# A hybrid decoder block on one core: 28 gate tiles as fourteen pairs by seven block products, recurrence operands read from DRAM, the inverse of four heads at a time

## The chip, the core and the metric

The kernel runs on one core of one Trainium2 chip. TensorE (PE) multiplies matrices into PSUM; VectorE (DVE), ScalarE (ACT) and GpSimd (POOL) do the elementwise work; SyncE (SP) issues nearly all DMAs. Each engine runs its own instructions in the order in which the program wrote them, and waits for the others by semaphores. The metric is the device time of one execution in microseconds, as a median over runs.

## The reference, cut to what matters

One block works on 1024 tokens of width 1024. All of it is float32.

```python
h = rms_norm(x, norm_w) * (1 + scale) + shift            # scale, shift, gate from c @ ada_w
proj = h @ w_in                                           # one projection, split in columns:
(qa, ka, va, za, beta_in, a_in, qb, kb, vb, zb, ga, gb) = split(proj)
qa, ka, va = split(silu(causal_dwconv(concat(qa, ka, va))))
o_a = gated_delta_rule(l2(qa), l2(ka), va, g, beta)       # 8 heads of 128, a recurrence over chunks
y_a = (rms_norm(o_a) * silu(za)) @ w_proj_a
o_b = dilated_window_attention(qb, kb, vb)                # 12 heads of 64, three groups
y_b = (o_b * softmax_over_groups * silu(zb)) @ w_proj_b
merged = sigmoid(ga) * y_a + sigmoid(gb) * y_b
out = rms_norm(x + gate * (merged @ w_out), final_norm_w)
```

The four quantities `za`, `zb`, `ga` and `gb` are the gates. They need nothing but `h` and their columns of `w_in`, and they are used late.

## The kernel before

**Products.** A float32 product is made of three: each operand is split into a high part `hi`, rounded to the type float32r, and the rest `lo`, and `three` (line 557) sums hi·hi, hi·lo and lo·hi. The activations stand transposed in eight pairs of tiles `hT[kk]` of 128 x 1024 (128 features by all tokens). A projection tile is 128 columns of `w_in`: for each of eight `kk` six matmuls of 512 columns, 48 in all, into one of two PSUM tiles `pj` of two banks. There are 66 such tiles: 8 each of q, k, v and z of mixer A (`qA`, `kA`, `vA`, `zA`), 6 each of `qB`, `kB`, `zB`, and 16 of the gates `gA` and `gB`. The three value tiles `vB` have the tokens in the rows and are made of 192 matmuls of 272 or 256 columns each. Behind the projections, `tail_products` (line 1532) multiplies by P_A (8 tiles of 48), P_B (8 of 36) and W_o.

**Weights.** `w_load` (line 521) brings a tile into one of two buffers `wr`; `w_split` (line 529) makes `hi` on ACT and `lo` on DVE in two of six tiles `wh`; the raw buffer is free again when both are made.

**Order.** The program is written by a planner. Every piece of work is a generator, a stream; `Sched` (line 103) keeps a clock for each engine with estimated durations (`book`, line 120) and lets the ready stream of the lowest number write its next instructions. The stream `projections` (line 724) has the number 99: it fills PE whenever no other stream has something ready. So the order on every engine is fixed before the run. `ORDER` (line 27) gives the projection tiles in four rounds of two heads each, with `g` for a gate tile; then come `qB` and `kB`, the six `zB` and what is left of the gates.

**Space.** 34 `big` tiles of 128 x 1024 hold `hT` (16), the operands of the heads in work, and the rest; six `mid` tiles of 128 x 512 and four one-bank PSUM tiles `sb` serve the smaller streams. `Slots.get` waits for a free tile.

**Mixer A.** For a head: `conv` (k, q, v), `d_stream` (decay), `k_stream` (k by rows, scaled: `KP`), `n_stream` (the 8 triangular matrices of 128 x 128), `inv_stream` (line 949), `merge_stream` (line 977), `q_stream`, and `rec_stream` (line 1107). `inv_stream` inverts the 32 x 32 diagonal blocks of two heads, 64 partitions, by 31 multiplications and 31 subtractions on DVE; `merge_stream` joins them to the inverse `TT`, of which there are two. `rec_stream` goes through eight chunks, each with matmuls that need the result of the one before, and reads k, q, `KP`, v and the matrix `AT` from tiles in SBUF. `turn` (line 1082) moves tokens back to the free axis through DRAM.

**Mixer B.** `attn_group` (line 1271) loads a group's values, waits for the group before, and has two workers go through eight `attn_unit` (line 1191). `combine` (line 1316) takes the softmax over the groups when all three are done and `ev_yas[7]` is set; `apply_gate` multiplies with the gate; `yb_split` makes the parts for P_B.

At the start `FIRST` (line 24) is 2: the tiles k0 and k1 are computed while `h` is being formed, and `ORDER` goes on with q0 and B0.

## Time and profile before

| what | us |
|---|---|
| median of 3 runs (1300.20 to 1302.47) | 1302.35 |
| the profiled execution | 1300.81 |
| its span, first to last instruction | 1299.0 |
| PE busy | 1261.6 |
| DVE, ACT, POOL busy | 690.9, 494.3, 145.4 |
| mean granted TensorE clock | 0.994 of full speed |

A page of the profile gives the busy time of each engine, the span in 40 slices of 32.5 us with the busy share in tenths, the chain of work that ended last, followed back from the last instruction, and groups of instructions with their count, busy time, mean duration and the idle time ahead of them. Every operation is recorded by one helper (line 96), so that groups are told apart by the names of their tiles: `pj<-big,wh` is a projection matmul, `wh<-wr` the splitting of a weight, `sb<-` the small streams. Matmuls overlap in the pipeline: the mean duration of one is longer than the distance between two. Other views are lists of waits by engine, tables of busy time in stretches of the span, and the timeline, in which a row is start, duration, engine and instruction, with a count where several follow each other.

### The profile page before, as it was taken

The page shows a single profiled execution, that of the slowest core. Times are in us where ns is not written, and L with a number is a line of the kernel's source. Part 1 is how long each engine was busy: PE and PEld are TensorE (multiplying, and loading weights), DVE is VectorE, ACT ScalarE, POOL GpSimd, SP SyncE. Part 2 cuts the span into 40 slices and gives each one's busy share as a digit, 9 for nine tenths or more (in the row PEclk, how much of TensorE's full clock was granted, in tenths as well). Part 3 has the DMA queues.
Part 4 walks back from the last instruction along what each step waited for, and adds up shares of the span by engine and source line. Part 5 has one row for each costly group of instructions (what it writes and reads, how often), then busy time and mean ns, then how long its engine had stood idle before and what let it go on. Part 6 is the DMA issues. An engine that isn't in the chain of part 4 may idle for free.

```text
span 1299.0 us, 18858 instructions
## 1 busy us (share of the span) xinstructions
PE 1261.6 (97%) x7386; PEld 1049.0 (81%) x7386; DVE 690.9 (53%) x1437; ACT 494.3 (38%) x1054; POOL 145.4 (11%) x97
## 2 busy tenths in 40 slices
PE   5799899999999999999999999999999999999997
PEld 3698678988888988888888888777777888888886
DVE  6766682377763468843778533232322147645433
ACT  5637312455234362234542242453536342222211
POOL 4601200023000221001310002000000000002400
PEclk9899999999999999999999999999999999999999
DMA  9335532163321433231522226211100257333422
GB/s 362 120 123 179 95 93 58 33 197 94 95 70 40 149 125 93 78 102 33 179 74 73 82 66 194 66 35 65 35 33 33 83 187 208 102 127 117 156 95 89
DMA packets 76138, 137.65 MB, mean 106 GB/s; under 512 B 30193, under 2 KB 43921, under 8 KB 76050
## 3 DMA queue, kind: packets, MB, share of 16 engines
q1 hardware_dynamic: 75906, 136.20, 33.2%
q8 instruction: 58, 0.95, 0.3%
q14 instruction: 30, 0.25, 0.1%
q10 hardware_dynamic: 144, 0.26, 0.1%
HBM read 105.84 MB, written 30.59 MB: 105 GB/s over the span
## 4 chain that ended last, share of the span: by engine, by line
PE 82%; issue 7%; DVE 6%; DMA 3%; POOL 1%; ACT 1%; SPq 0%; POOLq 0%; DVEq 0%; ACTq 0%
PE pj L96 69%; PE sb L96 13%; DVE big L96 4%; DMA big<-in_x_dram 1%; DMA vtd<-big 1%; DVE wh L96 1%; POOL big L96 1%; DVE mod L96 1%; DMA big<-grow 0%; ACT big L96 0%; DVE mid L96 0%; DMA big<-otd 0%; SPq L96 0%; POOL mo L96 0%; DMA otd<-big 0%
## 5 line engine op out<-in xcount | busy, mean ns | idle before, releaser
L96 PE MATMUL pj<-big,wh 128*128 128x512 f32 x3840 | 941.8, 398 | 11.2 <-POOL big L96 6.4
L96 PEld LDWEIGHTS pj<-big,wh 128*128 128x128 f32 x3840 | 706.3, 189 | 157.5 <-POOL big L96 7.8
L96 ACT ACTIVATE wh<-wr 128x1024 fp32r<-128x1024 f32 (+3 forms) x96 | 95.6, 996 | 316.1 <-PE pj L96 292.4
L96 DVE TENSOR_TENSOR wh<-wr,wh 128x1024 fp32r<-128x1024 f32 (+3 forms) x93 | 115.5, 1243 | 148.1 <-ACT wh L96 147.9
L96 ACT ACTIVATE big<-big 128x1024 f32<-128x1024 f32 (+1 forms) x61 | 64.5, 1059 | 147.2 <-DVE big L96 115.7
L96 PE MATMUL pj<-wh,big 128*128 128x256 f32 (+2 forms) x702 | 109.5, 307 | 0.0
L96 PEld LDWEIGHTS pj<-wh,big 128*128 128x128 f32 x702 | 95.9, 189 | 5.2 <-DVE big L96 0.2
L96 DVE SCALAR_TENSOR_TENSOR big<-pj,cw,big 128x1023 f32<-128x1023 f32 (+2 forms) x66 | 84.4, 1279 | 1.8 <-ACT big L96 0.3
L96 PEld LDWEIGHTS sb<-sq,big 128*128 128x128 f32 x464 | 62.6, 191 | 4.4
L96 PE MATMUL sb<-sq,big 128*128 128x128 f32 x464 | 65.5, 274 | 0.0
L96 DVE TENSOR_TENSOR big<-big,big 128x1024 f32<-128x1024 f32 (+3 forms) x40 | 55.2, 1388 | 15.1 <-ACT big L96 13.0
L96 ACT ACTIVATE big<-pj 128x1024 f32<-128x1024 f32 (+1 forms) x56 | 51.7, 923 | 21.3 <-PE pj L96 21.2
L96 ACT ACTIVATE mid<-sb 128x384 f32<-128x384 f32 (+5 forms) x75 | 34.1, 461 | 66.8 <-PE sb L96 66.4
L96 POOL TENSOR_TENSOR wh<-wr,wh 128x1024 fp32r<-128x1024 f32 x3 | 8.4, 2785 | 399.0 <-ACT wh L96 399.0
L96 ACT ACTIVATE mid<-mid,sta 128x128 f32<-128x128 f32 (+1 forms) x96 | 42.2, 441 | 25.5 <-DVE sta L96 25.4
L96 DVE COPY big<-sb 128x256 f32<-128x256 f32 (+1 forms) x32 | 12.4, 389 | 74.0 <-PE sb L96 73.9
L96 DVE SCALAR_TENSOR_TENSOR sq<-sq,gsm,sb 128x128 f32<-128x128 f32 x48 | 16.5, 345 | 63.2 <-PE sb L96 61.8
L96 PE MATMUL pj<-big,big 128*128 128x512 f32 x210 | 49.1, 389 | 0.0
L96 ACT ACT_TABLE_LOAD x29 | 37.2, 1283 | 28.8 <-DVE big L96 23.9
L96 PE MATMUL sb<-big,big 128*128 128x128 f32 (+4 forms) x365 | 45.5, 316 | 2.0 <-DVE big L96 2.0
L96 PEld LDWEIGHTS pj<-big,big 128*128 128x128 f32 x210 | 39.4, 188 | 8.2
L96 DVE TENSOR_TENSOR mid<-big 64x31 f32<-64x31 f32 (+15 forms) x124 | 41.1, 332 | 9.0 <-POOL big L96 5.6
(124 smaller groups left out, 1086.3 us busy)
## 6 DMA issues: line engine op xcount, KB each, us to landing
wr<-in_w_tiles_dram SPq DMA_DIRECT2D x64, 512.0 KB, 3.9
big<-in_ada_w_dram SPq DMA_DIRECT2D x24, 512.0 KB, 9.0
big<-in_x_dram SPq DMA_DIRECT2D x16, 512.0 KB, 5.0
gd<-big SPq DMA_DIRECT2D x16, 512.0 KB, 5.0
big<-gd SPq DMA_DIRECT2D x16, 512.0 KB, 4.7
big<-grow SPq DMA_DIRECT2D x8, 512.0 KB, 5.6
vtd<-big SPq DMA_DIRECT2D x8, 512.0 KB, 3.0
big<-vtd SPq DMA_DIRECT2D x32, 128.0 KB, 3.8
```

The lines of the kernel that those rows point to most:

```text
L96: r = f(*a, **k)
```

## The change

**Pairs.** The gate tiles `zA` (8), `zB` (6) and the first 14 of `gA`, `gB` are made two at a time (`two`), each pair by a form of Strassen's algorithm (`pair`). The weights of two tiles and the activations are cut into 2 x 2 blocks, A and B: halves of the features by tile, and halves of the features by halves of the tokens. Seven products of 128 x 512 x 512 give the four output blocks, where S1 = A21 + A22, S2 = S1 - A11, S3 = A11 - A21, S4 = A12 - S2, T1 = B12 - B11, T2 = B22 - T1, T3 = B22 - B12, T4 = B21 - T2. A product is four steps of three matmuls, 84 for the pair. `w_combine` makes the sums of the weights, `h_blocks` those of the activations once; T1 takes the place of B12 in `hT` and B12 comes back from DRAM after the last pair. `pair_out` adds the products up, and the outputs, through Silu or Tanh, go to DRAM (`z_d`, `gate_d`).

**Order.** The pairs come after 15 entries of `EARLY` (`a` is a `qB` and a `kB` tile) and ahead of `ORDER`, which has the other heads, the other attention tiles and two plain gate tiles; `named` and `ATT` hold attention group 0 until head 3's last chunk is loaded, 1 until k6, 2 until v7. The first tile behind k0 and k1 is B0.

**DRAM.** k, q, `KP` and `AT` are written to `rk_d`, v to `vr_d`, the triangular matrices to `nr_d`; `rec_stream` reads one chunk of 128 x 512 at a time into the two halves of one tile (`chunks`, two ahead). The q and k of mixer B go through `qb_d` and `kb_d`, read half a group at a time (`attn_second`), attention outputs through `og_d`; `yb_split`, two streams, reads them with the gates and takes over `apply_gate`; `combine` no longer waits for `ev_yas[7]`.

**Other.** `inv_stream` takes four heads, 128 partitions, twice instead of four times. The low part of a plain weight tile is made by POOL in place of DVE. The load of the last eight `ada_w` tiles begins when `h` is done. In `Sched.book` the estimates change (for a large matmul `n / 2.4 + 13.4` in place of `max(107, n / 2.4 + 2)`, and larger constants for DVE, ACT, POOL and the DMAs, a smaller one in `chain`).

The core of the diff:

```diff
-ORDER = (
-    "q0 B0 v0 q1 v1 z0 g g z1 g g B1",
-    "k0 k1 q0 v0 z0 g v1 q1 z1 g g B2",
-    "k0 k1 q0 v0 z0 g q1 v1 g g z1 g",
-    "k0 k1 q0 v0 z0 g q1 v1 z1 g g g",
-)
+EARLY = "k0 k1 B0 k2 k3 q0 q1 q2 q3 v0 v1 v2 v3 a0 a1"
+ORDER = "k4 k5 k6 k7 q4 q5 q6 q7 v4 v5 B1 a2 v6 v7 a3 B2 a4 a5 g14 g15"
+HALVES = (slice(0, 512), slice(512, 1024))
+PRODUCTS = (("A11", "B11"), ("S2", "T2"), ("S1", "T1"), ("A12", "B21"), ("S3", "T3"), ("S4", "B22"), ("A22", "T4"))
+BLOCKS = ("B11", "T2", "T1", "B21", "T3", "B22", "T4")
+ATT = ("c3", "k6", "v7")
+BLK = "q1"
+NTWO = 14
...
             yield
-            dve.tensor_tensor(u.lo, u.raw, u.hi.bitcast(F32), op=OP.subtract)
+            pool.tensor_tensor(u.lo, u.raw, u.hi.bitcast(F32), op=OP.subtract)
             wr.put()
             S.set(u.ev)
             yield S.now()
...
+    def w_combine(u):
+
+        half = u.n // 2
+
+        def part(src, names, hi, lo):
+            n = half * len(names)
+            act.activation(hi[:, 0:n], src, AF.Copy)
+            yield
+            dve.tensor_tensor(lo[:, 0:n], src, hi[:, 0:n].bitcast(F32), op=OP.subtract)
+            for q, name in enumerate(names):
+                sl = slice(q * half, q * half + half)
+                u.part[name] = (hi[:, sl], lo[:, sl])
+                S.set(u.ev[name])
+            if names[0] == "S2":
+                big.put()
+                big.debt += 1
+            if names[0][0:2] in ("S3", "S4"):
+                wr.put()
+
+        def begin(src, *names):
+            if len(names) == 2:
+                hi = yield from wh.get(F32R, shape=[P, u.n])
+                lo = yield from wh.get(F32R, shape=[P, u.n])
+            else:
+                t = yield from wh.get(F32R, shape=[P, u.n])
+                hi, lo = t[:, 0:half], t[:, half:]
+            S.add(part(src, names, hi, lo), 2, f"part{names[0]}")
+            yield S.now()
+
+        def sums():
+            yield u.raw_ev[1]
+            pool.tensor_tensor(s1, a21, a22, op=OP.add)
+            dve.tensor_tensor(s2, s1, a11, op=OP.subtract)
+            S.set(ev_s2)
+            yield ev_s2
+            pool.tensor_tensor(a21, a11, a21, op=OP.subtract)
+            S.set(ev_s3)
+            yield u.ev["A12"]
+            pool.tensor_tensor(a11, a12, s2, op=OP.subtract)
+            S.set(ev_s4)
+
+        ss = yield from big.get(owed=1)
+        s2, s1 = ss[:, 0:half], ss[:, half:2 * half]
+        ev_s2, ev_s3, ev_s4 = Event(), Event(), Event()
+        yield lambda: u.raws
+        a11, a12 = u.raws[0][:, 0:half], u.raws[0][:, half:]
+        yield u.raw_ev[0]
+        yield from begin(u.raws[0], "A11", "A12")
+        yield u.raw_ev[1]
+        a21, a22 = u.raws[1][:, 0:half], u.raws[1][:, half:]
+        S.add(sums(), 2, "sums")
+        yield ev_s2
+        yield from begin(ss[:, 0:u.n], "S2", "S1")
+        yield ev_s3
+        yield from begin(u.raws[1], "S3", "A22")
+        yield ev_s4
+        yield from begin(a11, "S4")
 
...
+    def pair(u, blocks, ready, sink, free=None):
+
+
+
+        nk = u.n // 2 // P
+        ps = {}
+        done = {b: Event() for _, b in PRODUCTS}
+        S.add(pair_out(ps, done, sink), 8, "pairout")
+        for n, (a, b) in enumerate(PRODUCTS):
+            if n in (0, 2):
+                two = yield from pj.get()
+            if n > 3:
+                pt = yield from sb.get()
+            else:
+                pt = two[:, HALVES[n % 2]]
+            ps[b] = pt
+            yield u.ev[a]
+            w, v = u.part[a]
+            for kt in range(nk):
+                yield ready[b][kt]
+                whi, wlo = w[:, kt * P:(kt + 1) * P], v[:, kt * P:(kt + 1) * P]
+                hi, lo = blocks[b][kt]
+                pe.matmul(pt, whi, hi, start=kt == 0, stop=False)
+                pe.matmul(pt, whi, lo, start=False, stop=False)
+                pe.matmul(pt, wlo, hi, start=False, stop=kt == nk - 1)
+                if free:
+                    free(b, kt)
+                yield S.now()
+            if a in ("S1", "A12", "A22"):
+                wh.put(2)
+            elif a == "S4":
+                wh.put()
+            S.set(done[b])
+
+    def pair_out(ps, done, sink):
+        def add(o, x, y):
+            dve.tensor_tensor(o, x, y, op=OP.add)
+
+        yield done["B11"]
+        p, u, v = yield from mid.many(3)
+        act.activation(p, ps["B11"], AF.Copy)
+        yield done["T2"]
+        add(u, p, ps["T2"])
+        pj.put()
+        yield done["T1"]
+        add(v, u, ps["T1"])
+        yield done["B21"]
+        add(p, p, ps["B21"])
+        pj.put()
+        yield
+        yield from sink(0, 0, p)
+        yield done["T3"]
+        add(p, v, ps["T3"])
+        add(u, u, ps["T3"])
+        sb.put()
+        yield
+        yield from sink(1, 1, p)
+        mid.put()
+        yield done["B22"]
+        add(v, v, ps["B22"])
+        sb.put()
+        yield
+        yield from sink(0, 1, v)
+        mid.put()
+        yield done["T4"]
...
+
+    HB = {b: [None] * 4 for b in BLOCKS}
...
+    def h_blocks():
+
+        def whole(o, kk, q):
+            hi, lo = (x_[:, HALVES[q]].bitcast(F32) for x_ in hT[kk])
+            pool.tensor_tensor(o, hi, lo, op=OP.add)
+
+        def sub(o, x_, y):
+            dve.tensor_tensor(o, x_, y, op=OP.subtract)
+
+        def part(name, i, src):
+            yield lambda: len(big.free_at) > big.debt + 1
+            t = yield from big.get(F32R, add=0)
+            hi, lo = t[:, HALVES[0]], t[:, HALVES[1]]
+            act.activation(hi, src, AF.Copy)
+            yield
+            pool.tensor_tensor(lo, src, hi.bitcast(F32), op=OP.subtract)
+            HB[name][i] = (hi, lo)
+            S.set(ev_hb[name][i])
+
+        yield [ev_h[kk][q] for kk in range(8) for q in range(2)]
+        yield named(BLK)
+        for i in range(4):
+            for b, kk, q in (("B11", i, 0), ("B21", i + 4, 0), ("B22", i + 4, 1)):
+                HB[b][i] = tuple(x_[:, HALVES[q]] for x_ in hT[kk])
...
+            whole(m1, i, 1)
+            whole(m2, i + 4, 1)
+            sub(m3, m2, m1)
+            yield
+            yield from part("T3", i, m3)
+            whole(m3, i, 0)
+            sp.dma_start(b12_d[i], m1)
+            sub(m1, m1, m3)
+            sp.dma_start(t1_d[i], m1)
+            sub(m2, m2, m1)
+            mid.put()
+            yield
+            yield from part("T2", i, m2)
+            whole(m3, i + 4, 0)
+            sub(m3, m3, m2)
+            mid.put()
+            yield
+            yield from part("T4", i, m3)
+            mid.put()
+
+        big.debt += 1
+        yield ev_early1
+        for i in range(4):
+            m1 = yield from mid.get()
+            sp.dma_start(m1, t1_d[i])
+            S.add(t1_part(i, m1), 1.5, f"t1{i}")
+            yield S.now()
+        for i in range(4):
+            yield ev_t1free[i]
+            m1 = yield from mid.get()
+            sp.dma_start(m1, b12_d[i])
+            yield
+            hi, lo = (x_[:, HALVES[1]] for x_ in hT[i])
+            act.activation(hi, m1, AF.Copy)
+            yield
+            dve.tensor_tensor(lo, m1, hi.bitcast(F32), op=OP.subtract)
+            mid.put()
+            S.set(ev_b12[i])
+
+    def t1_part(i, m1):
+        yield ev_last[i]
+        hi, lo = (x_[:, HALVES[1]] for x_ in hT[i])
+        act.activation(hi, m1, AF.Copy)
+        yield
+        pool.tensor_tensor(lo, m1, hi.bitcast(F32), op=OP.subtract)
+        mid.put()
+        HB["T1"][i] = (hi, lo)
+        S.set(ev_hb["T1"][i])
+
+    ev_early1 = Event()
+    ev_last = [Event() for _ in range(4)]
+    ev_t1free = [Event() for _ in range(4)]
+    ev_b12 = [Event() for _ in range(4)]
+
...
+    def block_sink(dst, ev, func, scale):
+
+        left = [2, 2]
+
+        def sink(r, q, src):
+            act.activation(src, src, func, scale=scale)
+            yield
+            sp.dma_start(dst[r][:, HALVES[q]], src)
+            left[r] -= 1
+            if not left[r]:
+                S.set(ev[r])
+
+        return sink
 
 
...
+    def two(base, dst, ev, func, scale):
+        for i in range(0, len(dst), 2):
+            prog.append(("two", block_sink(dst[i:i + 2], ev[i:i + 2], func, scale),
+                         w_pair(w_tiles[base + i], w_tiles[base + i + 1], T)))
+
+    plain(EARLY)
+    NEARLY = len(prog)
+    two(24, z_d[0:8], ev_zd[0:8], AF.Silu, 1.0)
+    two(44, z_d[8:14], ev_zd[8:14], AF.Silu, 1.0)
+    two(50, gate_d[0:NTWO], ev_gate, AF.Tanh, 0.5)
+    LAST2 = len(prog) - 1
+    plain(ORDER)
...
+    def keep(h, part, src):
+
+        sp.dma_start(rk_d[h][:, :, part * P:(part + 1) * P], src.rearrange("p (c f) -> p c f", c=8))
+        S.set(ev_rk[h][part])
+
...
     def inv_stream(p):
-        yield [ev_n[2 * p], ev_n[2 * p + 1]]
-        xx = yield from big.get(owed=1)
+        yield ev_n[4 * p:4 * p + 4]
+        xx = yield from big.get()
         tm = yield from mid.get()
-        xv = xx[0:64, :]
...
         for j in range(31):
             a, w = 31 - j, j + 1
-            tv = tm[0:64, 0:a * w].rearrange("p (k l) -> p k l", k=a)
-            dve.tensor_tensor(tv, x3[:, j, j + 1:, None].to_broadcast([64, a, w]),
-                              x3[:, j:j + 1, 0:w].to_broadcast([64, a, w]), op=OP.mult)
+            tv = tm[:, 0:a * w].rearrange("p (k l) -> p k l", k=a)
...
+    def chunks(h, t):
+
+        for c_ in range(8):
+            yield lambda: c_ < used[h] + 2
+            sl = t[:, HALVES[c_ % 2]]
+            sp.dma_start(sl, rk_d[h][:, c_])
+            CK[h, c_] = [sl[:, q * P:(q + 1) * P] for q in range(4)]
+            S.set(ev_ck[h][c_])
+            yield S.now()
 
...
+        yield [ev_mn[h], *ev_rk[h]]
+        ot = yield from big.get(add=1)
+        ct = yield from big.get(owed=1)
+        sp.dma_start(ot, vr_d[h])
+        S.add(chunks(h, ct), 3 + h * 0.01, f"chunks{h}")
+        yield ev_T[h]
...
         st = None
         for c_ in range(8):
+            yield ev_ck[h][c_]
+            kt, qt, kp, at = CK[h, c_]
             i = h * 8 + c_
-            sl = slice(c_ * P, (c_ + 1) * P)
             if c_:
                 pb = yield from sb.get()
```

428 lines of the change are left out of this document (270 added, 158 removed).

## The prediction

> **What bounds the kernel now.** I read the page from the top: busy shares, slices, then the chain that ended last.
>
> ```profile
> span 1299.0 us, 18858 instructions
> ...
> PE 1261.6 (97%) x7386; PEld 1049.0 (81%) x7386; DVE 690.9 (53%) x1437; ACT 494.3 (38%) x1054; POOL 145.4 (11%) x97
> ...
> PE   5799899999999999999999999999999999999997
> ...
> PEclk9899999999999999999999999999999999999999
> ...
> PE 82%; issue 7%; DVE 6%; DMA 3%; POOL 1%; ACT 1%; SPq 0%; POOLq 0%; DVEq 0%; ACTq 0%
> ```
>
> TensorE is busy for 97% of the span and makes 82% of the chain; only the first two slices and the last are short of full. A busy PE need not be at its peak, so the next question is what one matmul costs where nothing disturbs it. The pieces of the chain and the grouped lines answer that.
>
> ```profile
> 1083.51 197.31 PE pj L96 x870
> ...
> 1280.83 5.46 PE sb L96 x24
> ```
> ```profile
> L96 PE MATMUL pj<-big,wh 128*128 128x512 f32 x3840 | 941.8, 398 | 11.2 <-POOL big L96 6.4 <-ACT big L96 1.8 <-DVE wh L96 1.6
> ```
>
> In the tail 870 matmuls of 512 columns follow each other in 197.31 us: 226.8 ns each (the mean of 398 ns in the group overlaps its neighbours). The 24 in the second piece are a 512-wide piece of the last output tile, accumulated into one bank with the weights changing as they will in the block products: 5.46/24 = 227.5 ns. So the new order costs the old price per matmul. The count checks: 66 projection tiles of 48, eight of 48 for P_A and eight of 36 for P_B make 3840. They go on through the span; no other engine limits it. What PE loses is in its waits and in one stretch of windows.
>
> ```profile
> PE sb L96 <- DVE big L96: 8.0, 6, 2.1
> PE pj L96 <- POOL big L96: 6.4, 4, 2.3
> PE sb L96 <- DVE qpart L96: 4.7, 1, 4.7
> ```
> ```profile
> 150.00:155.00 5.00, 3.41 (x22) 2.88 (x23) 4.96 (x11) 0.00 (x0) 0.00 (x0) 1.00 0.37 104
> 155.00:160.00 5.00, 4.16 (x18) 2.81 (x16) 4.93 (x9) 2.95 (x4) 0.00 (x0) 1.00 0.32 80
> 160.00:165.00 5.00, 1.08 (x10) 0.96 (x11) 4.79 (x17) 0.67 (x2) 0.15 (x1) 0.91 0.39 144
> 165.00:170.00 5.00, 5.00 (x18) 3.99 (x18) 4.83 (x13) 0.00 (x0) 0.00 (x0) 0.75 0.53 159
> ```
>
> Columns: window, PE busy, PEld, DVE, ACT, POOL, granted clock, DMA. Three of the windows lose 1.59 + 0.84 + 3.92 = 6.35 us, and the clock of 0.91 and 0.75 after them takes 0.45 + 1.25 us more: 8 us, the only sizeable hole behind the start.
>
> **The change, part by part.** *Block products.* Two plain tiles are 96 matmuls; seven products of four steps of three are 84. Fourteen pairs save 168, at 226.8 ns: **-38.1 us**. No matmul is added elsewhere. This comes off the engine that sets the end, so it stays unless PE waits for something new.
>
> *Weights of a pair.* Rows for its steps:
>
> ```profile
> L96 ACT ACTIVATE wh<-wr 128x1024 fp32r<-128x1024 f32 x75 | 79.3, 1058 | 246.8 <-PE pj L96 225.3 <-issue 17.8 <-DMA wr<-in_w_tiles_dram 2.6
> L96 DVE TENSOR_TENSOR wh<-wr,wh 128x1024 fp32r<-128x1024 f32 x72 | 97.3, 1351 | 134.9 <-ACT wh L96 134.7
> ...
> L96 POOL TENSOR_TENSOR big<-wr,big 128x1024 fp32r<-128x1024 f32 x5 | 12.0, 2404 | 11.0 <-ACT big L96 6.0 <-PE pj L96 5.0
> ...
> L96 DVE TENSOR_TENSOR big<-mid,big 128x512 fp32r<-128x512 f32 x16 | 10.5, 690 | 9.5 <-ACT big L96 9.4
> L96 ACT ACTIVATE big<-mid 128x512 fp32r<-128x512 f32 x16 | 9.4, 626 | 9.9 <-DMA mid<-yad 9.8
> ...
> L96 POOL TENSOR_TENSOR big<-big,big 128x512 f32<-128x512 f32 x1 | 1.5, 1512 | 3.2 <-ACT mid L96 3.2
> ```
> ```profile
> wr<-in_w_tiles_dram SPq DMA_DIRECT2D x64, 512.0 KB, 3.9
> ```
>
> Seven half-size weight blocks take seven wh tiles; there are six. S4 gets its tile only when the product S1 ends. Its copy and subtraction (0.63 + 0.69) free the raw tile for the next pair's second load (3.9), then come POOL's sum (1.51), DVE's difference (0.69), the 1024-wide copy (1.06) and subtraction (1.35): 9.8 us to the next pair's S2 and S1. PE needs S2 after A12, S3, S4, A22 and the next A11: 5 x 12 x 226.8 ns = 13.6 us, more where other streams' matmuls lie between. Slack is 3.8 us a pair. It can be eaten: DVE and ACT run in order, and an add of pair_out or a step of an inverse may stand ahead. Bounds for the fourteen pairs: nothing, or all waits together (below: 78 us). The nearest row is the plain weights' own: PE waited for DVE wh 1.6 us in all. That chain had more room, so I take 0.7 us a pair: **+10 us**.
>
> What the pair's outputs add to DVE (seven 512-wide adds, 4.8 us of each 19.05 us pair) and to ACT (one copy, four activations of 0.63) lies beside the products; without that cover the first two banks would be held, and the next pair starts 8 us after its fourth product, which is the margin.
>
> *POOL takes the plain tiles' low parts* (2.40 us, against DVE's 1.23 undisturbed), once in a tile of 10.9 us: nothing in steady state. The forming of T1 to T4 is 32 POOL operations of 1.51 us, 48 us in the some 110 us between q1 and the first pair. A shortage of big tiles there bounds it at 0 to 10 us; I take 0, since ten plain tiles cover it.
>
> *B0 comes straight after k0 and k1.*
>
> ```profile
> 76.58 14.45 PE L96 MATMUL pj<-wh,big 128*128 128x272 f32 x114
> ```
> ```profile
> 76.33 0.66 ACT L96 ACTIVATE wh<-wr 128x544 fp32r<-128x544 f32 x1 [0.68 <-PE pj L96]
> ```
>
> Its third weight piece was copied as q0 ended, and B0 followed without a gap, at 126.8 ns a matmul; one piece feeds 18 matmuls of the first pass, 2.3 us. Now two pieces remain when k1 ends: the second needs about 0.9 + 1.9 us (POOL's row, scaled to 816 columns). Late by 0.5 to 4: **+1**.
>
> *The return of B12 after the last pair* runs four rounds one behind the other: load, copy, subtraction.
>
> ```profile
> xd<-big SPq DMA_DIRECT2D x4, 256.0 KB, 3.0
> ...
> mid<-yad SPq DMA_DIRECT2D x16, 256.0 KB, 5.4
> ```
>
> A round is 3.0 to 5.4, plus 1.32; four are 17 to 27 us. From T1's first free block to the fourth step of k4 are 2.0 + 10.9 + 4.1 = 17 us. Late by 0 to 10: **+3**, once.
>
> *The hole at 150 to 165 us* was DVE, 99% busy, with the first inverse and the q sums ahead of what PE wanted. That order is gone; a new one may have its own. Bounds -8 to +8; the stretch is now plain tiles, so I take **-4**.
>
> *Inverse of four heads.*
>
> ```profile
> L96 DVE TENSOR_TENSOR big<-big,mid 64x31 f32<-64x31 f32 (+15 forms) x124 | 41.6, 335 | 4.2
> L96 DVE TENSOR_TENSOR mid<-big 64x31 f32<-64x31 f32 (+15 forms) x124 | 41.1, 332 | 9.0 <-POOL big L96 5.6
> ```
>
> Twice the partitions and half the instructions: 41 us less of DVE, none of it on the path: 0.
>
> *Operands through DRAM* add some 84 MB to 138 and about 250 SP issues. The waits stand on SP's queue:
>
> ```profile
> SPq L96 <- DVE wh L96: 542.9, 63, 29.7
> ```
>
> SP stood 543 us waiting to reload a weight tile and PE hardly felt it. New there are 64 chunk loads, the later ones waiting for the matmuls of the chunk two before; behind them wait weight loads. The recurrence took eight chunks of two heads in this time, first and last:
>
> ```profile
> 740.32 0.31 ACT L96 ACTIVATE junk<-big 128x128 f32<-128x128 f32 x1 [1.63 <-DVE big L96]
> ...
> 785.75 0.31 ACT L96 ACTIVATE junk<-big 128x128 f32<-128x128 f32 x1 [2.08 <-DVE big L96]
> ```
>
> About 6 us a chunk, against a 512 KB load in 3.9: hidden. At 8 us a chunk heads 6 and 7 would end 16 us later; after v7 come eight plain tiles and a value tile, 87 + 24 us, before they are needed. Cost 0; at worst it delays weights, which the bound above holds.
>
> Sum, on the profiled execution's 1300.8 us (span 1299.0 and 1.8 around it; the median shown is 1302.35): 1300.8 - 38.1 + 10 + 1 + 3 - 4 = 1272.7. **Forecast 1273 us.** Its own range is 1256 (no stall in the pairs, the whole hole gone) to 1286.
>
> **Rivals.** *First: DVE and POOL get in each other's way in the pairs.*
>
> ```profile
> 279.82 2.41 POOL L96 TENSOR_TENSOR big<-big,cst 128x1024 f32<-128x1024 f32 x1
> ...
> 281.06 2.25 DVE L96 TENSOR_TENSOR wh<-wr,wh 128x1024 fp32r<-128x1024 f32 x1
> ```
> ```profile
> 1019.41 1.23 DVE L96 TENSOR_TENSOR wh<-wr,wh 128x1024 fp32r<-128x1024 f32 x1 [3.58 <-ACT wh L96]
> ```
>
> The same subtraction took 2.25 us beside POOL and 1.23 alone: it ended 1.1 us after POOL did, as if it had begun only then. The weight chain has three DVE steps and one of POOL; if each meets one operation of the other, it grows by up to 3 x 1.5 + 1.4 = 5.9 us, and with a conv of three shifted sums ahead (3.9 us) the chain is late by 5.9 + 3.9 - 3.8 = 6.0 us, 78 us in 13 handovers; at half of both it is late by 1.1 us. This rival is a stall of 1.7 to 2.9 us a pair: 1286 to 1304, middle 1293. The Trainium skill, "SBUF — State Buffer", section "Who interferes with whom", says that a VectorE instruction with two SBUF inputs and a GpSimd instruction that reads SBUF exclude each other, the later one waiting until the first is done; the trace agrees (2.25 against 1.23 us). By that rule the move of work to POOL is not free, and the time would be this rival's.
>
> *Second: the end of attention is late.*
>
> ```profile
> 962.46 0.29 DVE L96 CUSTOM_DVE_ANT_0 mid<-sb,cst 128x128 f32<-128x128 f32 x1 [1.04 <-PE sb L96]
> ...
> 1015.41 0.42 DVE L96 COPY big<-sb 128x256 f32<-128x256 f32 x1 [6.94 <-PE sb L96]
> ```
> ```profile
> 1071.83 1.84 DVE L96 TENSOR_TENSOR mid<-mid 128x32 f32<-128x32 f32 x10
> ...
> 1083.75 0.69 DVE L96 TENSOR_TENSOR big<-mid,big 128x512 f32<-128x512 f32 x1 [1.45 <-DMA mid<-fgd]
> ```
>
> Group 2 took 53 us and the combining 12. Its last keys now come two tiles (22 us) before the tail; with its trip through DRAM (12) it ends 17 to 43 us into the tail, and six gated tiles in two streams take 45 to 54 more. P_B begins 87 us in and asks for all six within 8: late by 0 to 15 us: 1273 to 1288, middle 1281. Against it: half of the group can begin a tile earlier.
>
> *Third, the other side: the weight chain decides every handover.* Slower than 1305 needs (1305 - 1262.7)/14 = 3.0 us of stall in each pair, four fifths of it beyond forecast. The place is S2 of each pair; the price at 4 us is 1319. It decides once the chain passes 16.6 us, so if loads land in 5 to 9 us, as SP holds them behind chunk loads, and blocking adds its half. For it speaks DVE at 99% in the windows above; against it, PE has the other streams' matmuls to do meanwhile.
>
> *Fourth: the products don't save.* If the blocks cost more per matmul, 1302; the 227.5 ns speak against it.
>
> **How the numbers follow.** Forecast 0.55; first rival 0.20; second 0.10; third 0.12; fourth 0.02; better than 1256 0.01. A measurement of this kernel can tell about 0.2% from no change: 1299.7 to 1305.0. Faster: 0.55 + 0.15 + 0.10 + 0.01 = 0.81; within: 0.05 of the first rival and the fourth, 0.07; slower 0.12. The range for 8 in 10 takes the forecast's case, the second, and the first up to 1298: 1256 to 1298.
>
> **What would show it.** Right: 3840 large matmuls become 3672, 512-wide ones still some 227 ns, PE idle up by 10 us or so between 250 and 600, waiting for DVE or ACT wh. Wrong: holes of 3 us at each S2 (first and third rival), PE waiting for DVE wh past 40 us in all, or a hole before P_B (second).

## The result, and the profile after

The changed kernel takes 1337.4 us (median of 4 runs, 1335.76 to 1340.84), the kernel before 1301.65 us (4 runs, 1300.2 to 1302.47): ratio 1.0279, 95% interval 1.0255 to 1.0304. The forecast was 1273 us, with a range of 1256 to 1298; the time lies 39 us above the top of that range. The span is 1334.6 us, 35.6 more than before.

The changed kernel's page, its totals, two rows of the slices and the first line of the chain:

```profile
span 1334.6 us, 19368 instructions
...
PE 1252.5 (94%) x7218; PEld 1028.3 (77%) x7218; DVE 749.5 (56%) x1412; ACT 532.1 (40%) x1140; POOL 382.6 (29%) x227
...
PE   5798899989999899999989999999999999999997
...
PEclk9899899989999999999989999999999999999999
...
PE 42%; DVE 4%; DMA 2%; issue 1%; ACT 0%; SPq 0%; POOL 0%; POOLq 0%; DVEq 0%; ACTq 0%
```

There are 168 matmuls fewer, as counted; but PE's row has five slices at 8 where it had one, and the granted clock dips to 8 in four slices where it did in one. What PE waited for, from the list of its waits (us in total, times, longest), and the groups of the large matmuls:

```profile
PE pj L106 <- DVE big L106: 13.5, 6, 8.6
PE pj L106 <- DVE mid L106: 12.5, 14, 2.4
PE pj L106 <- ACT mid L106: 8.6, 11, 1.4
PE pj L106 <- POOL big L106: 8.6, 6, 2.3
...
PE pj L106 <- ACT big L106: 5.9, 3, 2.9
...
PE pj L106 <- POOL wh L106: 1.1, 1, 1.1
PE pj L106 <- DVE wh L106: 1.1, 1, 1.1
```
```profile
L106 PE MATMUL pj<-big,wh 128*128 128x512 f32 x3168 | 806.8, 404 | 48.1 <-DVE mid L106 12.5 <-DVE big L106 11.6 <-ACT mid L106 8.6
L106 PE MATMUL sb<-big,wh 128*128 128x512 f32 x504 | 130.0, 402 | 0.2 <-DVE mid L106 0.2
```

3168 + 504 = 3672 large matmuls. The waits for weights (`wh`) are 2.2 us in all. The new ones are for `mid` tiles, 21.1 us in 25 pieces: DVE's and ACT's work on the pairs' *outputs*. In the list of before no `mid` stood among the first rows. The chain's shares add up to half of the span only, so I don't use it here.

To see where the time went, I take for each matmul the distance from its start to the next one's, less the usual distance of its shape (227 ns for 512 columns, else the median in the trace of before), and sum by stretch. This counts waits and half clock alike. "B12" is the 48 large matmuls behind the last pair; "attention" the 150 us that begin 330 us ahead of the last matmul. One profiled execution stands for each kernel. The rows named e1 to e12 are the kernels of the next section.

```
lost us        0-60   to 1st pair  1st pair  pairs 2-14   B12   to att.  attention  rest    sum
before         30.9      12.8      (9.7 from 277 to 700 us)      15.5       5.8     -0.2    74.5
before+row(e5) 31.6       3.7      (9.7 from 277 to 700 us)      15.5       5.7     -0.3    66.0
plain (e3)     32.1      18.7      (12.9 from 277 to 700 us)     17.6      15.1      0.4    96.8
after          30.9      16.1        12.1       47.2      8.6    18.5      14.4      0.4   148.2
tiles (e1)     30.2      16.1         7.6       33.0      9.4    18.3      13.5      0.4   128.5
row (e2)       31.6       5.1        12.9       52.3      7.8    18.6      13.9      0.4   142.6
POOL->DVE (e6) 30.2      21.8        20.3       49.7      9.6    17.1      10.7      0.5   159.9
e4_both        30.5       5.1         9.7       30.3      0.0    18.2      15.2      0.4   109.4
e8_blkq0       30.1      13.7        14.5       28.2      0.0    19.1      14.3      0.5   120.4
e9_sinkq       30.2      13.0        14.8       20.8      0.0    18.0      13.9      0.3   111.0
e10_q          30.0       5.1         7.4       28.8      0.0    18.2      13.9      0.3   103.7
e11_v7         30.2       5.1         7.5       28.5      0.0    21.4      28.4      0.4   121.5
e12_v67        30.2       5.2         7.5       31.9      0.0    19.7      30.6      0.4   125.5
```

After less before is 73.7 us of loss; less the 38.1 us of the 168 matmuls this is 35.6, the difference of the spans. So the products' gain arrived whole, and almost twice as much was given back: 58.2 us in the pairs with what follows them (12.1 + 47.2 + 8.6 against 9.7), 8.6 at the end of attention, 3.3 ahead of the first pair, 3.6 elsewhere. Three places show how.

**Inside a pair.** Timeline of the changed kernel in the fifth pair, loads of weights left out (start, duration, engine, instruction, idle time before it and its releaser):

```profile
409.57 0.96 PE L106 MATMUL pj<-big,wh 128*128 128x512 f32 x3
...
410.57 0.69 DVE L106 TENSOR_TENSOR mid<-mid,pj 128x512 f32<-128x512 f32 x1 [3.20 <-PE pj L106]
...
411.31 0.50 PE L106 MATMUL pj<-big,wh 128*128 128x512 f32 x1 [0.78 <-DVE mid L106]
```

The first row ends the third product. DVE's add reads its bank, and the fourth product, which writes the *other* bank of the same `pj` tile, begins when the add has ended (411.26). Ahead of the second product PE waits likewise for ACT's copy of the first. In all fourteen pairs there are 25 such waits.

**Ahead of the first pair.** The same kernel, SP's timeline, then DVE's and PE's:

```profile
113.68 0.38 SPq L106 DMA_DIRECT2D rowd<-mod  x1
114.16 1.78 SPq L106 DMA_DIRECT2D big<-grow  x2
```
```profile
128.28 5.16 DVE L106 TENSOR_TENSOR_SCAN big<-big,cst 128x128 f32<-128x128 f32 x16 [14.63 <-DMA big<-grow]
```
```profile
138.10 9.14 PE L106 MATMUL pj<-big,wh 128*128 128x512 f32 x30 [8.63 <-DVE big L106]
```

The write of `rowd`, 4.0 KB, is issued half a microsecond ahead of two loads of decay rows; DVE's scan has to wait 14.63 us for them, the conv of k3 stands behind the scan, its `pj` tile isn't freed, and PE stops for 8.63 us. The table of DMA issues (the last figure is the median us to landing) and the windows (PE, PEld, DVE, ACT, POOL busy, clock, DMA share, GB/s) show what the queue did meanwhile:

```profile
big<-grow SPq DMA_DIRECT2D x8, 512.0 KB, 6.5
...
rowd<-mod SPq DMA_DIRECT2D x1, 4.0 KB, 9.3
```
```profile
115.00:120.00 5.00, 5.00 (x24) 4.12 (x23) 0.00 (x0) 4.88 (x15) 0.00 (x0) 1.00 0.15 10
...
130.00:135.00 5.00, 0.00 (x0) 0.00 (x0) 4.90 (x16) 3.96 (x12) 1.19 (x1) 0.73 0.03 9
135.00:140.00 5.00, 1.90 (x5) 1.54 (x6) 4.86 (x6) 4.91 (x9) 4.65 (x4) 0.50 0.26 85
```

10 GB/s at a DMA share of 0.15: the transfers stand behind the little write. In the kernel before, the same write was issued at 130.30, ahead of `vtd<-big`. The clock falls inside the hole (0.73 from 130 to 135 us, in which PE did nothing) and is still at 0.50 when PE goes on. The Trainium skill, "TensorE: Matmul & The Clock Gate", Part 1, says that the clock is halved after an idle window of some 3.4 us and restored after a busy one, and that the windows run freely; the trace agrees on the clock (0.50), and its stretches of half clock between 60 and 1300 us last 3.4, 6.8 or 10.2 us each. It doesn't agree that a whole window has to be idle: in the 3.50 us ahead of the half clock at 514.6 PE was busy for 1.50.

**First pair and B12.** Rows of PE in the changed kernel, the first pair and the return of B12:

```profile
286.25 0.80 PE L106 MATMUL pj<-big,wh 128*128 128x512 f32 x1 [2.53 <-ACT big L106]
287.67 5.61 PE L106 MATMUL pj<-big,wh 128*128 128x512 f32 x11 [0.63 <-POOL big L106]
295.65 4.61 PE L106 MATMUL pj<-big,wh 128*128 128x512 f32 x12 [2.37 <-DVE mid L106]
```
```profile
677.58 0.73 PE L106 MATMUL pj<-big,wh 128*128 128x512 f32 x2 [2.94 <-ACT big L106]
680.04 15.21 PE L106 MATMUL pj<-big,wh 128*128 128x512 f32 x55 [1.73 <-DVE big L106]
```

In the first pair `big` is block T1, its high part (ACT) and then its low part (POOL): the third product waits for them. In the second fence it is B12's high and low parts. The third row is another wait: for DVE's add of this pair's own output. DVE had the inverse of four heads to do at that time, its steps in between the work on the blocks and the pair, and the add came when the last of them was done:

```profile
261.64 1.39 DVE L106 TENSOR_TENSOR mid<-big 128x252 f32<-128x252 f32 x1
...
263.52 0.42 DVE L106 TENSOR_TENSOR mid<-big 128x255 f32<-128x255 f32 x1
...
294.80 0.19 DVE L106 TENSOR_TENSOR big<-big,mid 128x31 f32<-128x31 f32 x1
294.91 0.69 DVE L106 TENSOR_TENSOR mid<-mid,pj 128x512 f32<-128x512 f32 x1
```
```profile
259.87 2.88 POOL L106 TENSOR_TENSOR mid<-big,big 128x512 f32<-128x512 f32 x2
```

`mid<-big` and `big<-big,mid` are steps of the inverse. One took 1.39 us beside POOL's sums for the blocks, and the next of its kind 0.42 us with POOL idle.

### The profile page after: what moved, and what is told of

Same layout as the page of the kernel before. It is cut to its first block, busy times and chain, and to the rows that moved or that the text cites. A ratio compares the mean times of both kernels' runs of the same rounds, so it can differ in the third digit from the quotient of the medians.

```text
span 1334.6 us, 19368 instructions
## 1 busy us (share of the span) xinstructions
PE 1252.5 (94%) x7218; PEld 1028.3 (77%) x7218; DVE 749.5 (56%) x1412; ACT 532.1 (40%) x1140; POOL 382.6 (29%) x227
## 5 line engine op out<-in xcount | busy, mean ns | idle before, releaser
L106 PE MATMUL pj<-big,wh 128*128 128x512 f32 x3168 | 806.8, 404 | 48.1 <-DVE mid L106 12.5
L106 PEld LDWEIGHTS pj<-big,wh 128*128 128x128 f32 x3168 | 587.6, 192 | 182.2 <-DVE mid L106 18.0
L106 POOL TENSOR_TENSOR wh<-wr,wh 128x1024 fp32r<-128x1024 f32 (+4 forms) x64 | 145.4, 2273 | 446.9 <-ACT wh L106 389.3
L106 ACT ACTIVATE wh<-wr 128x1024 fp32r<-128x1024 f32 (+4 forms) x110 | 104.2, 948 | 157.7 <-PE pj L106 112.5
L106 PE MATMUL sb<-big,wh 128*128 128x512 f32 x504 | 130.0, 402 | 0.2 <-DVE mid L106 0.2
L106 PEld LDWEIGHTS sb<-big,wh 128*128 128x128 f32 x504 | 91.3, 189 | 19.3 <-DVE mid L106 1.2
L106 PEld LDWEIGHTS sb<-sq,big 128*128 128x128 f32 x464 | 65.0, 190 | 12.1 <-issue 3.2
L106 DVE TENSOR_TENSOR mid<-mid,pj 128x512 f32<-128x512 f32 x42 | 28.8, 687 | 61.7 <-PE pj L106 57.3
L106 POOL TENSOR_TENSOR big<-mid,big 128x512 fp32r<-128x512 f32 x32 | 50.5, 1584 | 37.5 <-ACT big L106 22.3
L106 DVE TENSOR_TENSOR wh<-wr,wh 128x1024 fp32r<-128x1024 f32 (+1 forms) x46 | 51.9, 1131 | 7.4 <-ACT wh L106 7.2
L106 DVE TENSOR_TENSOR mid<-mid,sb 128x512 f32<-128x512 f32 x56 | 37.0, 682 | 33.3 <-DMA zd<-mid 14.3
L106 ACT ACTIVATE mid<-mid 128x512 f32<-128x512 f32 (+1 forms) x59 | 35.9, 609 | 47.7 <-DVE mid L106 47.3
L106 ACT ACTIVATE mid<-mid,sta 128x128 f32<-128x128 f32 (+1 forms) x96 | 42.1, 440 | 27.0 <-DVE sta L106 26.9
```

What stands on the lines that cost most here:

```text
L106: r = f(*a, **k)
```

## The experiments

The kernel before was run beside each group, at medians of 1301.02 to 1301.19 us, so the times can be set side by side.

**One part alone: the tiles.** In `pair`, products 1 and 2 begin in two different `pj` tiles and 3 and 4 follow in the other halves; `pair_out` frees both later.

```diff
-            if n in (0, 2):
-                two = yield from pj.get()
+            if n < 2:
+                two[n] = yield from pj.get()
...
-                pt = two[:, HALVES[n % 2]]
+                pt = two[n % 2][:, HALVES[n // 2]]
```

> The changed kernel with one edit: the first four products of a pair alternate between the two pj tiles (P1 and P3 in one, P2 and P4 in the other), so that two neighbouring products never share a tile. Theory (PE's 0.9 us gaps ahead of the second and the fourth product are waits for ACT's and DVE's reading of the other half of the same tile): both gaps go, 14 x (0.92 + 0.95) = 26 us, and some half-clock stretches behind them: 1337 to about 1311 (1303 to 1316). Rival A (a product's end has to reach DVE or ACT before PE may go on, whichever tile it is in): the gaps stay, 1337 within 4. Rival B (the gaps go, but PE then waits for the weights or the banks of the next pair): gaps of 2 us appear ahead of S2 or P1 and the time stays above 1325.

Measured 1318.43 us (1316.04 to 1320.69), ratio 1.0136 (1.0114 to 1.0157): 19.0 us less than the changed kernel. Its list of PE's waits:

```profile
PE pj L106 <- DVE big L106: 12.2, 4, 8.7
PE pj L106 <- POOL big L106: 8.8, 6, 2.3
...
PE pj L106 <- ACT big L106: 8.2, 3, 4.3
...
PE pj L106 <- ACT wh L106: 4.6, 1, 4.6
```

The rows for `mid` under `pj` are gone. No bank was added: only which products share a tile. The instructions stand in the changed kernel's order on all four engines. The time is a little above the theory's range; one wait of 4.6 us for weights has come up (the second pair's S2), the sign that rival B named. The Trainium skill, "Perfetto Trace Analysis", section "Matmuls", says that groups of matmuls should rotate through PSUM banks so that reading one overlaps filling the next. Here consecutive products did lie in different banks and PE waited all the same; in this program the waits go by tile.

**The row alone.** The write of `rowd` waits for the first gate tile.

```diff
-        sp.dma_start(row_d.rearrange("o (j p) -> p (o j)", p=P), mod[:, 16:24])
         big.put()
+        yield ev_zd[0]
+        sp.dma_start(row_d.rearrange("o (j p) -> p (o j)", p=P), mod[:, 16:24])
```

> The changed kernel with one edit: the write of the gate row (1024 single elements, 4 KB) waits until the first gate pair is out, in place of standing just ahead of the two loads of the decay rows. Theory (that write holds the DMA queues for some 10 us, the decay row lands after 14 us in place of 6, DVE's scan waits 14.6 us with the convolution of k3 behind it, and PE lacks a bank for 8.6 us, then runs at half clock for 10 us): the hole at 129 us goes, 9 to 14 us less, 1323 to 1328. Rival (the hole comes from the row write's neighbours, the k tiles going to DRAM on SP's queue ahead of the loads): the hole stays, 1337 within 4.

Measured 1329.47 us (1325.43 to 1334.91), ratio 1.0219 (1.0189 to 1.0249). The hole goes, and DVE's scan waits 2.26 us for the same loads: the theory, though the time is a little above its range. The stretch ahead of the first pair loses 5.1 us in place of 16.1, 11.0 less; 5.1 us come back in pairs 2 to 14 and a little elsewhere, so that 5.6 us remain between the two profiled executions and 7.9 between the medians.

**The same in the kernel before.** There the row waits for the first `qB` tile.

> The kernel before with one edit: its write of the gate row waits until the first qB tile is out. Theory (the row write holds the DMA queues in this kernel too: the write of v behind it took 11.3 us in place of 3, and the hole at 150 to 165 us, 8 us with the half clock, follows from it): 1302 to about 1293 (1290 to 1296). Rival (that hole is DVE's load alone, the first inverse and the q sums): the same within 2 us.

Measured 1292.07 us (1291.93 to 1292.74), ratio 0.9930 (0.9915 to 0.9945). The stretch to 277 us loses 3.7 us in place of 12.8. Thus the old hole at 150 to 165 us, which the prediction put down to DVE's load, was at bottom this write.

**The change without the products.** The 28 gate tiles as plain tiles at the same place, their outputs through the same DRAM tensors; everything else of the change stays.

```diff
+            if kind == "one":
+                pt = yield from pj.get()
+                yield u.ev
+                for kk in range(8):
+                    yield from three(pt, u.hi[:, kk * P:(kk + 1) * P], u.lo[:, kk * P:(kk + 1) * P], *hT[kk], kk == 0, kk == 7)
```

> The changed kernel with its 28 gate tiles as plain tiles of 48 matmuls at the same place, through the same DRAM buffers, without the blocks of h and without the sums of weights; all else as it is. Theory (of the 74 us that the change lost, 58 lie in the pairs: the first pair's wait for its blocks 11, the two gaps of each pair and what follows 39, the return of B12 8): 168 matmuls more cost 38, and 58 go: 1337 + 38 - 58 = 1317 (1310 to 1325). Rival (the trips through DRAM, the order and POOL's low parts cost it, and the gaps are where they show): the 38 come on top and little goes: 1360 to 1375.

Measured 1322.88 us (1320.73 to 1323.4), ratio 1.0163 (1.0148 to 1.0178). So the new order, the trips through DRAM, the inverse of four heads and the move to POOL cost 21.7 us without any pair; by the table mainly the new hole and the end of attention (15.1 against 5.8). The pairs by themselves add 14.5 us, though they save 38.1.

**POOL's part undone.** The low parts of the plain weights go back to DVE.

> The changed kernel with one line put back: the low parts of the plain weight tiles are made by DVE as before, not by POOL. Theory (POOL's part costs about 1 us, by PE's waits for POOL wh and DVE wh of 1.1 us each): 1337 us, within 1332 to 1342. Rival (DVE and POOL keep each other out of SBUF often enough to matter, the first rival of the prediction): 1325 or less, as DVE's other steps get shorter; or, if DVE is the short engine in the plain stretch, 1343 or more.

Measured 1346.78 us (1345.77 to 1348.06), ratio 1.0350 (1.0335 to 1.0365), 9.4 us above the changed kernel. Theory (no difference) and rival (less) both fall; only the rival's last clause holds. In its first pair, which loses 20.3 us in place of 12.1, PE waits longer for work on DVE and behind it (at the second row DVE's add again stands behind steps of the inverse):

```profile
290.62 0.50 PE L106 MATMUL pj<-big,wh 128*128 128x512 f32 x1 [3.68 <-ACT mid L106]
...
309.00 3.25 PE L106 MATMUL pj<-big,wh 128*128 128x512 f32 x7 [5.54 <-DVE mid L106]
```

So in this change POOL's low parts are a gain. With the edit the planner writes another order on all four engines, so the 9.4 us are not the price of the moved subtractions alone; that part isn't separated.

**Together.** Tiles, row, and B12's four rounds as separate streams, all loading at once (`S.add(b12_part(i, m1), ...)` in place of the copy and subtraction in the loop).

> The changed kernel with the first four products of a pair alternating between two pj tiles, the row of rowd written only when the first gate tile is out, and the four rounds of B12's return as four separate streams instead of one behind the other. Theory (the terms are separate and add): from the 1318.4 us of the tiles alone, the late row takes off 8 (as it did alone) and the parallel return of B12 some 5 of its 8.3 us: 1305 us, between 1299 and 1312; the stretch 668 to 690 loses less than 4 us over nominal, against 8.3. Rival (the gains overlap, since a stall removed in one place comes back in the next in which the same work is late): 1313 or more. The rival to the B12 part alone: the return is bound by the loads on SP's queue and not by the chain of rounds, so that stretch still loses 7 or more.

Measured 1300.56 us (1292.82 to 1304.95, 10 runs), ratio 0.9993 (0.9974 to 1.0012). The gains add, and a little more: B12's stretch loses 0.0, the one ahead of the first pair 5.1. All that was lost against the kernel before is back, but not yet the gain.

**Blocks earlier.** `BLK = "q0"` on top of that.

> e4_both with one constant changed: the blocks T1 to T4 begin to be formed when q0 is made and not when q1 is (BLK). Theory (the 11 us that the first pair loses are the blocks that come too late, 32 POOL operations and their copies behind other work): one tile of 11 us earlier gives most of it back: 5 to 9 us less than e4_both, some 1298 us (1293 to 1303), and the first pair's stretch loses less than 5 us. Rival (the blocks take big tiles that the convs of q and v need, or POOL's and ACT's order keeps them late): the same time as e4_both within 2 us, or slower, with the loss at the same place or ahead of it.

Measured 1308.26 us (1305.98 to 1311.19), ratio 1.0055 (1.0037 to 1.0072): the rival. The first pair loses 14.5 us in place of 9.7, and 8.6 more are lost ahead of it. PE's waits at the start of the first pair and at its fourth product:

```profile
274.01 5.38 PE L106 MATMUL pj<-big,wh 128*128 128x512 f32 x14 [4.14 <-ACT big L106]
...
294.46 5.09 PE L106 MATMUL pj<-big,wh 128*128 128x512 f32 x12 [6.34 <-DVE mid L106]
```

Neither is a wait for a block; the blocks now come in time, and the loss comes back in another form. At 274.01 PE gets the bank that ACT has read out (`big<-pj`), and ACT had stood before that for DVE's difference of a block. At 294.46 it gets the bank for which DVE's add stood behind the inverse of four heads, whose steps fill DVE from 281.10 on:

```profile
271.47 0.63 ACT L106 ACTIVATE big<-mid 128x512 fp32r<-128x512 f32 x1 [8.18 <-DVE mid L106]
...
272.95 1.01 ACT L106 ACTIVATE big<-pj 128x1024 f32<-128x1024 f32 x1
```
```profile
293.54 0.22 DVE L106 TENSOR_TENSOR big<-big,mid 128x60 f32<-128x60 f32 x1
293.72 0.69 DVE L106 TENSOR_TENSOR mid<-mid,pj 128x512 f32<-128x512 f32 x1
```

So the rival is right in the time and in part in the cause: what it didn't name is the inverse. In e4_both it is block T1 that PE waits for (3.1 us at the third product). One piece of what holds it: in the chain ahead of T1, ACT's copy of a T2 part stands behind a weight copy that waits for PE, although DVE's difference was ready at 264.35.

```profile
265.62 1.06 ACT L106 ACTIVATE wh<-wr 128x1024 fp32r<-128x1024 f32 x1 [7.14 <-PE pj L106]
...
267.50 0.62 ACT L106 ACTIVATE big<-mid 128x512 fp32r<-128x512 f32 x1
```

**Another queue for the outputs.** `block_sink` issues its writes from ACT's queue, first with `BLK = "q0"`:

> e8_blkq0 with one line changed: the writes of the pairs' outputs to z_d and gate_d are issued from ACT's own queue in place of SP's. Theory (a write of a half tile stands on SP's queue behind loads that wait for their buffers; the mid tile isn't freed, DVE's next add waits for it, and S2's subtraction and copy stand behind that add): DVE's waits for the writes fall from 14.3 us to under 4, and what the pairs still lose at S2 goes: 3 to 8 us less than e8_blkq0. Rival (those waits are off the path, the pairs' rest loss is DVE's and ACT's own work): DVE's waits fall likewise, the time stays within 2 us, or grows by 1 to 3 as ACT now issues 56 transfers.

Measured 1304.91 us (1299.51 to 1307.38), ratio 1.0023 (1.0010 to 1.0036), 3.4 us less than e8_blkq0. Then without it:

> e4_both (blocks formed from q1 on, as in the changed kernel) with the pairs' outputs written from ACT's own queue in place of SP's. Theory (half-tile writes stood on SP's queue behind loads; DVE's adds and with them S2 waited for the mid tiles): the gaps of 2.9 and 3.8 us ahead of an sb product in the stretch 400 to 500 shrink as they did in e9_sinkq, that stretch loses 7 instead of 12.7, and the gap ahead of the second pair's S2 goes: 4 to 8 us less than e4_both, 1295 us (1291 to 1298), faster than before. Rival (e9_sinkq gained only against a kernel in which the writes were queued worse): 1299 to 1302, as e4_both.

Measured 1291.93 us (1286.55 to 1298.15, 6 runs), ratio 0.9928 (0.9906 to 0.9950): 8.6 us less than e4_both in the medians, 5.8 in the profiled spans, and faster than both the kernel before and the changed one. The order of the instructions is that of e4_both on all four engines, so the queue makes the difference. Of the three signs that I named, two came: the stretch 400 to 500 loses 7.4 us in place of 12.7, and its gaps fall from 2.9 and 3.8 us to 1.5 and 2.5. The one of 3.8 shows the theory. First e4_both: DVE's add waits for a write that SP issued late, and the step for which PE waits stands behind the add. Then e10_q:

```profile
483.91 7.44 SPq L106 DMA_DIRECT2D gd<-mid  x2
```
```profile
489.65 1.29 DVE L106 TENSOR_TENSOR mid<-mid,sb 128x512 f32<-128x512 f32 x2 [3.67 <-DMA gd<-mid]
490.85 0.34 DVE L106 SCALAR_TENSOR_TENSOR sq<-sq,gsm,sb 128x128 f32<-128x128 f32 x1
```
```profile
477.91 0.33 ACTq L106 DMA_DIRECT2D gd<-mid  x1
```
```profile
485.46 1.29 DVE L106 TENSOR_TENSOR mid<-mid,sb 128x512 f32<-128x512 f32 x2 [2.45 <-DMA gd<-mid]
```

The third did not: the gap at the second pair's S2 stays (2.1 and 1.9 us), and 2.2 us come at the tenth pair's, so that pairs 2 to 14 together lose only 1.5 us less; 2.3 us of the 5.8 lie in the first pair and 1.3 at the end of attention. Nor did DVE's waits for these writes (`zd` and `gd`) fall as I wrote for e9_sinkq: 26.9 us became 23.7, and from e8_blkq0 to e9_sinkq 21.0 became 28.4, while the time fell both times. So it isn't their sum that counts but what stands behind a single one. What brings the rest of the 5.8 us, outside the stretch 400 to 500, stays open.

**The end of attention.** On e10_q, v7 (then v6 and v7) made behind a4, so that group 2 starts earlier.

> e10_q with the tile v7 made behind a4 (and group 2 held until v6 only). Theory (the loss at the end of attention, 12 to 14 us between 1000 and 1150, comes from group 2 being started by a4 so late that its last units run with too little plain work beside them): group 2 starts 11 us earlier, the stretch loses 5 less: some 1290 us (1286 to 1294). Rival (head 7's recurrence, now 90 us later, takes the same engines in the same stretch, or P_A waits for head 7): the same as e10_q or up to 10 us slower, with PE waiting for DVE or ACT behind 1000.

> e10_q with both v6 and v7 behind a4, so that B2 and a4 come 22 us earlier (group 2 held until q7). By the theory on the end of attention: group 2 starts 22 us earlier and the stretch 1000 to 1150 loses 8 less than in e10_q: 1287 us (1282 to 1293), if the recurrence of heads 6 and 7, begun some 70 us later and 48 us long, is still done before P_A asks for it some 60 us later. Rival: the recurrence is late, P_A waits for heads 6 and 7 at its first two tiles, 5 to 25 us: 1298 to 1320.

Measured 1307.95 us (ratio 1.0046, 1.0030 to 1.0062) and 1310.58 us (1.0082, 1.0058 to 1.0106), 16.0 and 18.7 us more than e10_q: the theory falls both times. The second lies in its rival's range, the first 6 us above its rival's 10. In e11_v7 PE stops at a small product of `combine`, with the large products behind it in program order:

```profile
1068.64 0.39 PE L106 MATMUL sb<-cst,fga 128*32 128x128 f32 x1 [12.31 <-DVE fga L106]
```
```profile
1063.01 1.67 DVE L106 SCALAR_TENSOR_TENSOR big<-big,dnw,big 128x256 f32<-128x256 f32 x4 [7.53 <-DMA big<-otd]
```

DVE's step for that product stood behind head 7's output, which came 7.53 us late out of DRAM. An earlier group 2 was paid for with a later head 7. In e12_v67 PE waits 6.9 us for ACT and DVE within the first two tiles of P_A, the place that the rival named, and 5.6 us for `combine`.

## Why the prediction was wrong, point by point

The sum allowed the losses 10 us (10 + 1 + 3 - 4) against a gain of 38.1. They came to 73.7: 49.6 more in the pairs than before in the same time, 8.6 at B12, 8.6 at the end of attention, 6.9 elsewhere.

- **Products.** Right: 3672 large matmuls, and the products in `sb`, which waited 0.2 us in all, stand 227 ns apart in the median. The fourth rival falls.
- **The outputs of a pair "lie beside the products", with a margin of 8 us.** This is the step that failed first. I asked when the *next* pair needs the banks and not what the next *product of the same pair* waits for. Products 1 and 2, and 3 and 4, share a tile; each copy or add on the one held up the other, some 0.9 us in 25 places, at zero in the sum. Undone alone it is worth 19.0 us.
- **Weight chain, +10.** Not what cost the time: PE waited 2.2 us for `wh` in all. I named holes at each S2 as the sign of the first and third rival, and none came; the time is nevertheless above the third rival's bound, by other waits. But the waits at the banks had covered it: with the tiles mended, S2 has holes at the second pair (4.6 us in e1_tiles) and in e10_q at the second and tenth, 4.8 us in all.
- **T blocks, 0, with a bound of 10.** The first pair still loses 7.6 us when the tiles are mended. The place was named, the cause not: the trace shows the order on ACT and DVE, where weight copies and the inverse of four heads stand between the steps of the blocks, while POOL waits (5.9 us for ACT in e4_both).
- **B12, +3.** Right mechanism, size off: 8.6 us, inside its bound of 10. With the rounds side by side it is 0.0.
- **The hole, -4.** The old one did go, some 9 us, but it was one DMA's doing and came back elsewhere: 11 us ahead of the first pair. "The row write" was not in my list of moved steps, although the change moves the load of the last `ada_w` tiles and with it everything `ada_stream` issues. "Operands through DRAM cost 0" hid the same omission: I counted SP's issues and not what one of them does to those behind it.
- **POOL.** Taken at 0; it is a gain of 9.4 us, as the e6 run shows. The first rival (DVE and POOL in each other's way) had the wrong sign for the plain tiles. What it says of the engines is there, in the steps of the inverse (1.39 us beside POOL, 0.42 without); that DVE's relief is worth more than this is argued from the sum, not shown.
- **End of attention, the second rival.** A loss of 8.6 us more than before, within its 0 to 15, but by luck: its sign, a hole before P_B, didn't come. P_B begins at 1174 us, and the whole stretch from 1147 us to the end loses 0.4. The loss lies ahead of that, beside P_A, where PE stops for the last units (1.5 us for `mid` from ACT), for `combine` (1.9 us for `fga` from DVE), and runs at half clock. The plain variant has it too, so it belongs to the order and not to the pairs.
- **B0, +1.** PE waited 0.4 and 1.1 us in it: right within its bounds.
- **Inverse of four heads, 0.** "None of it on the path" does not hold in the first pair, where the fourth product waited 2.4 us for an add behind it (6.3 in e8_blkq0). Nor did DVE save 41 us: the steps took 82.7 us before and 59.5 in the changed kernel (48.8 in the plain variant, which forms no blocks). It was not undone by itself, so its price stays open.

Also open: pairs 2 to 14 of e10_q lose 28.8 us where the plain variant lost 9.8 in about the same time (308 to 669 us). It isn't spread evenly: the second pair alone loses 8.8, and the third, fourth, seventh, ninth and fourteenth less than 0.5 each. Eleven gaps over 0.4 us make 11.9 of it, where the plain variant has one: 4.8 for weights at S2 of two pairs, 4.0 in two for DVE's `sq` in the recurrence, the rest mostly for `mid` tiles. What is left is half clock and pieces of 0.05 to 0.2 us; the plain variant has such pieces too. No run undoes any of these alone.

## What to carry to other kernels

When an operation is cut into shorter pieces, list for each piece what frees the tile that the next piece writes, for the next piece and not only for the next round: here a wait of 0.9 us came in 25 places of fourteen pairs, and a pair takes some 28 us (thirteen from 308 to 669). When a step moves, list every DMA that its stream issues and what stands behind it on the queue. And a saving on the bounding engine is whole only if each new piece of side work has its place in the *order* of its engine; an engine at 56% or 40% busy says nothing of that.

## What the runs showed of the hardware that was not expected

A write of 4.0 KB, 1024 elements of four bytes each, took 9.3 to 12.2 us to land (12.2 in the kernel before) and held up 512 KB loads issued behind it: DVE waited 14.63 us for two that usually land in 6.5. Moved away, it is worth 9 us in the kernel before and 8 in the changed one. And a gap of a few microseconds costs more than itself: inside the one of 8.63 us began a stretch of 10.2 us at half clock that outlasted it, so that 11 us were lost in all. A gap of 2.0 us just ahead of 514.6 us was enough for 3.4 us at half clock. Last, a step of the inverse on DVE took 1.39 us while POOL worked and 0.42 with POOL idle.
